# Sums of weight blocks made in DRAM scratch by accumulating transfers ahead of their stages, and nine more two by two steps, in a one-core transformer layer

## The chip, the cores and the metric

The kernel runs on one core of a Trainium2 chip. The time is the device time of one execution in microseconds (us). The kernel before took 716.37 us, the median of three runs (715.84 to 717.23).

Engines are named as the profile names them: PE multiplies matrices, DVE, ACT and POOL work on vectors, SP only issues transfers. Each engine runs its own instructions in a fixed order; an instruction that waits holds up all that stand behind it on its engine.

## The reference

One layer on 512 positions of width 1024, in float32:

```python
h = rms_norm(x, norm_mix_g[l])
proj = h @ w_in[l]                       # conv B, C, in | q, k, v | forget logits | gates
u = causal_dwconv(cc * cin, conv_mix_w[l])
y_conv = (cb * u) @ w_out_conv[l]
o = forgetting_attention(q, k, v, log_f) # 8 heads of 64
y_attn = o @ w_out_attn[l]
gates = jax.nn.sigmoid(g_logit + b_gate[l])
x = x + (g_conv * y_conv + g_attn * y_attn) @ w_o[l]
h = rms_norm(x, norm_ffn_g[l])
up = causal_dwconv(h @ w_up[l], conv_ffn_w[l])
a, b = jnp.split(up, 2, axis=-1)
x = x + (jax.nn.silu(a) * b) @ w_down[l]
return rms_norm(x, norm_f_g)
```

The hidden width is 2816, so that w_down is 22 by 8 blocks of 128 by 128.

## The kernel before, in words

**Products in three passes.** Everything lies with features on the partitions. A float32 product is made of three matmuls in a rounded format: each operand is split into hi (rounded) and lo (the rest), and hi·hi, lo·hi and hi·lo are summed in PSUM. One matmul takes a weight block of 128x128 and 256 positions. A plain product of four weight blocks (2 output by 2 input blocks) with both halves of the positions takes 8 such triples, 24 matmuls.

**Steps.** A *step* replaces these 8 products by 7 (21 matmuls): it multiplies sums and differences of the four weight blocks by sums and differences of the four input pieces, and adds results in the outputs. Seven weight forms are needed: three are plain blocks (the P chunk), four are sums (the F chunk). Two steps make a *double*. `seven` (L729) runs a list of doubles: chunk P is 18 matmuls (12 with the hi weights, then 6 with the lo weights), chunk F is 24 (16, then 8). Steps are used for the branch gates of output blocks j = 3 to 7 (`GATES`, two doubles each), and in the down projection. That runs in two phases, each behind its part of the up projection: hidden blocks 0 to 11 (phase 0, input pairs q = 0 to 5, 12 doubles) and 12 to 21 (phase 1, q = 6 to 10, 5 doubles), `STEPS`. In the lists (i, q) is output pair i with input pair q. What steps leave out in phase 1 is done in plain matmuls (`PLAIN`): outputs 2, 3, 6 and 7, in chunks dp0 to dp5.

**The weight stream.** All weights come through one list of chunks, `stream`. For each chunk SP loads `raw_*` (512 KB for 1024 columns), ACT makes the hi half `wh_*` (L237), DVE the lo half `wl_*` = raw - wh (L241). `wh` and `wl` have two buffers each, so a half of the next but one chunk waits until PE has read the one that lies there. `split` (L217) makes one chunk's halves while PE works on the chunk ahead of it.

**The sums.** For an F chunk SP loads half of the pieces to `raw_F` (256 KB), POOL adds the other half by an accumulating transfer (L187), and two POOL additions (L179, L180) make the last four of its eight columns of blocks, from `raw_F` itself and from `raw_P`. `sums`, `adds` and `forms` place them. ACT's hi half of an F chunk so waits for POOL.

**Side work.** Combining a step's outputs (`gate_pair`, `combine`), making the sums of the inputs (`x_sums`, `x_split` for the gates; `t13`, `t24` and `hl` in `glu` for the down projection) and the squares of the last norm (`final_square`) are entered in a list `later`, with a chunk from which they may run and a cost. After each split `run_later` (L198) issues as much of it as a budget of microseconds allows, and `flush` issues what a following step needs. So the order on DVE and ACT is fixed in the program, by the splits and these budgets.

**Names.** `xt`, `xth`, `xtl` are the sums of the normed input for the gates, with hi and lo halves; `xgh`, `xgl` the plain ones. `p_ga`, `p_gb` are gates of plain matmuls, `yc`, `ya` the two branch projections of a block j (chunk mix j), `g*`, `mh`, `ml` the merged branches. `dn*` are the PSUM banks of steps, `go`, `ge`, `gh`, `gl` the hidden activations and their forms, `pd`, `pdA`, `pdB` plain outputs of the down projection, `x`, `cz`, `cu` what combining writes. q10 is the last input pair of phase 1: its activations are made last, just before the steps.

Of the kernel before, what the change touches and what calls it, by code (L numbers as in the profile page):

```python
# [8 lines left out]
F32 = mybir.dt.float32  # L9
# [4 lines left out]
P = 128  # L14
# [34 lines left out]
    (((2, 6), (2, 7)), ((2, 8), (2, 9)), ((0, 6), (0, 7)), ((0, 8), (2, 10)), ((0, 9), (0, 10))),  # L49
# [11 lines left out]
def block_kernel(ctx, tc, xT, vecs, wv, win, wmix, wo, wup, wst, wdp, outT):  # L61
# [56 lines left out]
    def step_chunks(n):  # L118
        return [(f"P{n}", wst[n, :, : 6 * P], 6 * P), (f"F{n}", wst[n, :, 6 * P :], D)]
# [17 lines left out]
    raws, parts, order = [], [], {}  # L137
    later = []
    held = dict.fromkeys(NRAW, 0)
    stage = {"add": 0, "sum": 0}  # L140
# [11 lines left out]
    def load(upto):  # L152
        for k in range(len(raws), min(upto, len(stream) - 1) + 1):
            nm, src, ncol = stream[k]
            tag = tag_of(k)
            if held[tag] == NRAW[tag]:
                return
            held[tag] += 1
            pool = wp if tag == "raw" else fp if tag == "rf" else mp
            raw = pool.tile([P, D], F32, tag=tag, name=f"raw_{nm}", bufs=NRAW[tag])  # L160
# [13 lines left out]
    def sums(k, n):  # L174
        while stage["sum"] <= min(k + n, stage["add"] - 1):
            a = stage["sum"]
            if tag_of(a) != "raw":
                f, p = (raws[x].rearrange("p (a b) -> p a b", b=P) for x in (a, a - 1))
                keep(nc.gpsimd.tensor_add(f[:, 4:6], f[:, 0:4:2], p[:, 1:6:3]))  # L179
                keep(nc.gpsimd.tensor_add(f[:, 6:8], f[:, 4:6], p[:, 2:6:3]))  # L180
            stage["sum"] += 1

    def adds():
        while stage["add"] < len(raws):
            a = stage["add"]
            if tag_of(a) != "raw":
                keep(nc.gpsimd.dma_start(raws[a][:, : 4 * P], stream[a][1][:, 4 * P :], accum_op=ALU.add))  # L187
            stage["add"] += 1

    def forms(k):  # L190
        if k >= ff0:
            sums(k, 3)
            adds()
        else:
            adds()
            sums(k, 2)
# [20 lines left out]
    def split(hl=None):  # L217

        k = len(parts)
        if k == len(stream):  # L220
            return
        nm, _, ncol = stream[k]
        load(k + (LOOK if len(raws) > KB else AHEAD))
        forms(k)
        if hl is None:
            hl = []
            for x in "hl":
                if k == 0:
                    wp.tile([P, PADW[x]], F32, tag=f"pad{x}", name=f"pad_{x}")
                hl.append(wp.tile([P, D], F32R, tag=f"w{x}", name=f"w{x}_{nm}", bufs=2)[:, :ncol])  # L230
        hi, lo = hl
        raw = raws[k]
        if k == 0:
            for cs in (slice(0, VW), slice(VW, S + H)):
                keep(nc.vector.tensor_copy(hi[:, cs], raw[:, cs]))
        else:
            ins = nc.scalar.activation(hi, raw, AF.Copy)  # L237
            order["hi"] = ins.ins
            if k < KB:
                keep(ins)  # L240
        ins = nc.vector.tensor_sub(lo, raw, hi.bitcast(F32))  # L241
        order["lo"] = ins.ins
        if k < KB:
            keep(ins)
        held[tag_of(k)] -= 1
        assert tag_of(k) == "raw" or stage["sum"] > k
        parts.append((hi, lo))
        run_later(k, {"u": 1.7, "P": 1.6, "F": 0.75, "i": 3.0, "m": 3.0}.get(nm[0], 3.5))
# [452 lines left out]
    n = len(units)  # L701
    for i in range(n + LA):
        if i < n:
            scores(*units[i])
        take = 1 if i < n + LA - 1 else len(fill)
        for _ in range(min(take, len(fill))):
            fill.pop(0)()
        if 0 <= i - LT < n:
            transp(*units[i - LT])
        if 0 <= i - LA < n:  # L710
            pr, e, qb = units[i - LA]
            if e == 1 and qb % 2 == 1:
                attend(pr, qb // 2)
    at.close()
# [14 lines left out]
    def seven(doubles, n0, sets, operand, goes_on=None, stays=None, done=None):  # L729
# [3 lines left out]
        for n, d in enumerate(doubles):  # L733
            for kind in "PF":
                prods = []
                for s_, (i, q) in enumerate(d):
                    for f, g, b, h in PROD:
                        if (f < 3) == (kind == "P"):
                            wants.setdefault(f"{kind}{n0 + n}", []).append(("q", q))
                            c = 3 * s_ + f if f < 3 else 2 * s_ + f - 3 if f < 5 else 4 + s_ + 2 * (f - 5)  # L740
                            prods.append((c, i, operand(q, g), b, h))
# [33 lines left out]
    mp = mg.enter_context(tc.tile_pool(name="mp", bufs=1))  # L775
    mh = mp.tile([P, KB, S], F32R, tag="mh", name="mh")
# [43 lines left out]
    k = [c[0] for c in stream].index("mix1")  # L820
# [153 lines left out]
    fp = ctx.enter_context(tc.tile_pool(name="fp", bufs=1))  # L974
    fp.tile([P, PADL], F32, tag="pad", name="pad_f")
# [118 lines left out]
    for ph, (j0, j1) in enumerate(PHASES):  # L1094
        if ph:
            flush()
            acc = ring(*X)
        for j in range(j0, j1):
# [32 lines left out]
    def plain(m, t, ks, p, opens, closes):  # L1131
        for k in ks:
            while (m, k) not in where:
                fetch(plain.c)
                plain.c += 1
# [4 lines left out]
    plain.c = 0  # L1140
    for m, b in ((2, 4), (3, 2)):
        flush((b,))
        p = bank(b, f"pd{m}")
        for k in kall:
            for t in range(2):
# [10 lines left out]
    pdA, pdB6, pdB7 = bank(3, "pdA"), bank(5, "pdB6"), bank(0, "pdB7")  # L1156
# [56 lines left out]
def _layout(i):  # L1213
# [45 lines left out]
    for w4, d in [(wga, d) for d in GATES] + [(wdn, d) for d in STEPS[0] + STEPS[1]]:  # L1259
# [3 lines left out]
        w = pick((1, 1), (0, 0), (0, 1)) + pick((1, 0), (1, 0)) + pick((1, 1), (0, 0))  # L1263
        wst.append(np.concatenate(w, axis=1))
# [37 lines left out]
```

## Time and profile before

| | before |
|---|---|
| median of three runs | 716.37 us |
| the profiled execution | 716.79 us |
| its span in the trace | 715.0 us |
| PE, instructions | 6069 |
| DVE busy | 511.3 us |
| ACT busy | 334.0 us |
| POOL busy | 203.2 us |
| moved by DMA | 84.11 MB |

The span reaches from the first to the last instruction of the trace; the profiled execution is 1.8 us longer, start and end around it. A row of the timeline has start, length, engine, source line, operation, output and inputs; a bracket at its end says how long the engine was idle before and what it waited for. Matmuls overlap: their lengths are longer than the distance from one to the next, which is what counts.

### The profile page before, as it was taken

How to read it: one execution, taken by the hardware profiler on the slowest of the kernel's cores; microseconds unless marked ns; L12 is line 12 of the kernel's file. 1: busy time of each engine (PE TensorE's matmuls, PEld its weight loads, DVE VectorE, ACT ScalarE, POOL GpSimd, SP SyncE). 2: the span in 40 equal slices, each digit the busy share in tenths (PEclk: the TensorE clock that was granted, in tenths of full speed). 3: DMA queues.
4: the chain of work that ended last, by engine and by line, in shares of the span. 5: the costliest groups of instructions: out<-in, count | busy, mean ns of one | idle time of the engine just before them, and what ended most of it. 6: DMA issues, size and time to landing. Idle time of an engine off the chain costs nothing. (4 is left out here: it accounts for less than half of the span.)

```text
span 715.0 us, 14660 instructions
## 1 busy us (share of the span) xinstructions
PE 702.8 (98%) x6069; PEld 697.8 (98%) x6069; DVE 511.3 (72%) x758; ACT 334.0 (47%) x521; POOL 203.2 (28%) x222
## 2 busy tenths in 40 slices
PE   9999999999999999999999999999999999999996
PEld 9999999999999999999999999999999999999995
DVE  6677667675478888864468777779794677878963
ACT  5665545544464444343344444445433344444542
POOL 5124424222113444433301011045640111116202
PEclk9999999999999999999999999999999999999998
DMA  7423213122452656653313333357863233246313
GB/s 246 160 76 105 75 61 89 60 61 88 137 159 67 169 136 148 200 172 122 96 60 119 94 103 101 96 131 173 203 165 118 89 100 108 89 128 147 103 31 118
DMA packets 31571, 84.11 MB, mean 118 GB/s; under 512 B 3824, under 2 KB 6512, under 8 KB 31504
## 3 DMA queue, kind: packets, MB, share of 16 engines
q1 hardware_dynamic: 24736, 70.63, 31.1%
q0 software_dynamic: 5360, 11.31, 8.2%
q10 hardware_dynamic: 1408, 1.24, 0.5%
q8 instruction: 47, 0.77, 0.4%
q14 instruction: 20, 0.16, 0.1%
HBM read 81.00 MB, written 2.10 MB: 116 GB/s over the span
## 5 line engine op out<-in xcount | busy, mean ns | idle before, releaser
L269 PE MATMUL p_up<-x1h,wh_up 128*128 128x256 f32 x536 | 104.5, 276 | 0.0
L269 PE MATMUL p_up<-x1l,wh_up 128*128 128x256 f32 x536 | 104.4, 276 | 0.0
L269 PE MATMUL p_up<-x1h,wl_up 128*128 128x256 f32 x536 | 104.3, 276 | 0.0
L237 ACT ACTIVATE wh_up<-raw_up 128x1024 fp32r<-128x1024 f32 x44 | 46.7, 1060 | 89.1 <-PE p_up L269 68.8
L269 PEld LDWEIGHTS p_up<-x1h,wh_up 128*128 128x128 f32 x536 | 80.8, 188 | 0.0
L269 PEld LDWEIGHTS p_up<-x1l,wh_up 128*128 128x128 f32 x536 | 80.7, 188 | 0.0
L269 PEld LDWEIGHTS p_up<-x1h,wl_up 128*128 128x128 f32 x536 | 80.6, 188 | 0.0
L241 DVE TENSOR_TENSOR wl_up<-raw_up,wh_up 128x1024 fp32r<-128x1024 f32 x44 | 53.8, 1223 | 20.6 <-ACT wh_up L237 20.6
L269 PE MATMUL p_in<-xgh,wh_in 128*128 128x256 f32 x288 | 56.9, 279 | 1.0 <-ACT wh_in L237 1.0
L269 PE MATMUL p_in<-xgl,wh_in 128*128 128x256 f32 x288 | 56.5, 277 | 0.0
L269 PE MATMUL p_in<-xgh,wl_in 128*128 128x256 f32 x288 | 56.4, 277 | 0.0
L1008 POOL TENSOR_TENSOR ge<-fu,fu 128x512 f32<-128x512 f32 x11 | 17.1, 1551 | 124.2 <-DVE fu L519 111.3
L995 DVE TENSOR_TENSOR fz<-p_up,rb_n 128x512 f32<-128x512 f32 x44 | 30.3, 690 | 30.1 <-PE p_up L269 30.0
L269 PEld LDWEIGHTS p_in<-xgh,wh_in 128*128 128x128 f32 x288 | 44.7, 188 | 1.9 <-ACT wh_in L237 1.2
L241 DVE TENSOR_TENSOR wl_F<-raw_F,wh_F 128x1024 fp32r<-128x1024 f32 x27 | 39.6, 1468 | 8.7 <-ACT wh_F L237 8.1
L237 ACT ACTIVATE wh_F<-raw_F 128x1024 fp32r<-128x1024 f32 x27 | 28.6, 1061 | 33.7 <-PE dn L287 14.3
L269 PEld LDWEIGHTS p_in<-xgl,wh_in 128*128 128x128 f32 x288 | 43.6, 188 | 0.0
L269 PEld LDWEIGHTS p_in<-xgh,wl_in 128*128 128x128 f32 x288 | 43.5, 188 | 0.0
L287 PE MATMUL p_up<-x1h,wh_up 128*128 128x256 f32 x168 | 40.3, 277 | 0.0
L287 PE MATMUL p_up<-x1l,wh_up 128*128 128x256 f32 x168 | 40.2, 276 | 0.0
L241 DVE TENSOR_TENSOR wl_in<-raw_in,wh_in 128x1024 fp32r<-128x1024 f32 x26 | 33.2, 1276 | 9.6 <-ACT wh_in L237 9.1
L241 DVE TENSOR_TENSOR wl_P<-raw_P,wh_P 128x768 fp32r<-128x768 f32 x27 | 31.7, 1174 | 7.7 <-ACT wh_P L237 7.6
(315 smaller groups left out, 2127.2 us busy)
## 6 DMA issues: line engine op xcount, KB each, us to landing
raw_up<-in_wup_dram SPq DMA_DIRECT2D x44, 512.0 KB, 3.6
raw_in<-in_win_dram SPq DMA_DIRECT2D x26, 512.0 KB, 3.5
raw_P<-in_wst_dram SPq DMA_DIRECT2D x27, 384.0 KB, 3.2
raw_F<-in_wst_dram SPq DMA_DIRECT2D x27, 256.0 KB, 3.1
raw_F<-in_wst_dram POOLq DMA_DIRECT2D x27, 256.0 KB, 4.8
raw_mix<-in_wmix_dram SPq DMA_DIRECT2D x8, 512.0 KB, 4.8
raw_wo<-in_wo_dram SPq DMA_DIRECT2D x8, 512.0 KB, 6.7
xt<-in_xT_dram POOLq DMA_DIRECT2D x4, 512.0 KB, 6.4
```

The costliest lines, as they stand in the source:

```text
L237: ins = nc.scalar.activation(hi, raw, AF.Copy)
L241: ins = nc.vector.tensor_sub(lo, raw, hi.bitcast(F32))
L269: keep(nc.tensor.matmul(out[:, cs], w, x[:, cs], start=start and i == 0 and c == 0, stop=stop and i == 2 and c == len(cut) - 1,))
L287: keep(nc.tensor.matmul(out, wl if x == 1 else wh, xl if x == 2 else xh, start=opens and bk not in seen, stop=closes and bk not in left,))
L995: nc.vector.tensor_mul(z, p, rb2)
L1008: keep(nc.gpsimd.tensor_mul(ge, a.rearrange(halves_of, h=2), b.rearrange(halves_of, h=2)))
```

## The change

1. **The sums move into DRAM.** `make_forms` groups doubles and gives each group six transfers in DRAM scratch: SP copies pieces from `wst` there, POOL adds others by accumulating transfers (three copies, three additions, each waiting for the one ahead). `slot`, called once in each of the 37 turns of the attention loop and once for each up-projection block, issues what is due: the sums of the gates' 12 doubles during the attention (6 groups of 2, four slots from one transfer of a group to the next), those of phase 0 and phase 1 during the up projection ahead of them (groups of 4, two slots apart). SP then loads an F chunk like any other, 512 KB. `sums`, `adds` and `forms` go: 27 accumulating transfers and 54 additions of POOL. 36 accumulating transfers of POOL take their place (18 in the attention, 9 in each up projection), on 256 or 512 rows each instead of 128.
2. **Gates in steps from block 2** (`GJ`): two more doubles instead of plain matmuls. Their `xt` sums start a chunk earlier (`mix0` for `mix1`).
3. **Output pair 1 of phase 1 in steps**: two more doubles and one single step, (1, 10), at the end; `PLAIN` keeps outputs 6 and 7 (chunks dp0 to dp2). The order of the doubles changes: (2, 10) stands in the third instead of the fourth.
4. Banks of the last part are renumbered, and `wst` is padded to one width.

```diff
@@ tables @@
-    (((2, 6), (2, 7)), ((2, 8), (2, 9)), ((0, 6), (0, 7)), ((0, 8), (2, 10)), ((0, 9), (0, 10))),
+    (((2, 6), (2, 7)), ((2, 8), (2, 9)), ((2, 10), (0, 6)), ((0, 7), (0, 8)), ((0, 9), (0, 10)))
+    + (((1, 6), (1, 7)), ((1, 8), (1, 9)), ((1, 10),)),
-GJ = 3
+GJ = 2
-PLAIN = [(m, k) for m in (2, 3, 6, 7) for k in range(*PHASES[1])]
-PCUTS = (0, 8, 16, 20, 28, 32, 40)
+PLAIN = [(m, k) for m in (6, 7) for k in range(*PHASES[1])]
+PCUTS = (0, 8, 12, 20)
+DOUBLES = GATES + STEPS[0] + STEPS[1]
+GROUPS = {"gate": (2, 4, 1), 0: (4, 2, 4), 1: (4, 2, 3)}
@@ load @@
-            elif tag != "raw":
-                keep(nc.sync.dma_start(raw[:, : 4 * P], src[:, : 4 * P]))
             else:
-                keep(nc.sync.dma_start(raw[:, :ncol], src))
+                keep(nc.sync.dma_start(raw[:, :ncol], src if tag == "raw" else made[src]))
...
-                keep(nc.gpsimd.tensor_add(f[:, 4:6], f[:, 0:4:2], p[:, 1:6:3]))
-                keep(nc.gpsimd.tensor_add(f[:, 6:8], f[:, 4:6], p[:, 2:6:3]))
...
-                keep(nc.gpsimd.dma_start(raws[a][:, : 4 * P], stream[a][1][:, 4 * P :], accum_op=ALU.add))
...
+    def make_forms(n0, n1, key):
+        size, step, shift = GROUPS[key]
...
+            m = len(DOUBLES[a]) * P
+            f = dr.tile([P, b - a, 4 * m], F32, tag=f"f{a}", name=f"f{a}")
+            w = wst[a:b].rearrange("n p c -> p n c")
+            x0, x1, x2 = w[:, :, 3 * m : 5 * m], w[:, :, 5 * m : 7 * m], w[:, :, 7 * m : 8 * m]
...
+            def put(dst, src):
+                return lambda: keep(nc.sync.dma_start(dst, src))
+            def add(dst, src):
+                return lambda: keep(nc.gpsimd.dma_start(dst, src, accum_op=ALU.add))
+            f0, f1, f2 = f[:, :, : 2 * m], f[:, :, 2 * m : 3 * m], f[:, :, 3 * m :]
+            ops = (put(f0, x0), add(f0, x1), put(f1, f[:, :, :m]), add(f1, x1[:, :, m:]), put(f2, f1), add(f2, x2))
+            todo_bg.extend((make_forms.slot + step * k + shift * g, op) for k, op in enumerate(ops))
...
+    def slot():
+        while todo_bg and todo_bg[0][0] <= make_forms.slot:
+            todo_bg.pop(0)[1]()
+        make_forms.slot += 1
@@ attention loop, up @@
+    make_forms(0, len(GATES), "gate")
     for i in range(n + LA):
+        slot()
...
         for s_ in range(2):
+            slot()
@@ gates @@
-    k = [c[0] for c in stream].index("mix1")
+    k = [c[0] for c in stream].index("mix0")
@@ the last part @@
-    for m, b in ((2, 4), (3, 2)):
...
-                plain(m, t, (k,), p[:, th[t]], t == 0, t == 1)
-        nc.vector.tensor_add(x1[:, m, :], p, x1[:, m, :])
-        later.append((0, 0.8, (), lambda m=m: final_square(m)))
...
-    fetch(3)
+    fetch(0)
-    fetch(4, [wx[:, a : a + 4 * P] for a in (80, 752)])
-    fetch(5)
+    fetch(1, [wx[:, a : a + 4 * P] for a in (80, 752)])
+    fetch(2)
```

**What moves on the engines.** Below, a row has the source line (in the kernel after, most lines stand 13 to 18 further down), the operation, output and inputs with their numbers, and the shape. P0, F0, P1, F1 are the four chunks of block j = 2 after the change (of j = 3 before it).

ACT after, from the split of chunk F0 of block 2 on:

```order
L250 ACTIVATE wh_F0_2883<-raw_F0_2719 128x1024
L918 ACTIVATE mh_2595<-g1_2743 128x512
L250 ACTIVATE wh_P1_2915<-raw_P1_2721 128x768
L250 ACTIVATE wh_F1_2943<-raw_F1_2723 128x1024
L831 ACTIVATE xth_2590<-xt_2589 128x1024 x2
L250 ACTIVATE wh_mix2_2975<-raw_mix2_2733 128x1024
```

DVE after, at the same place:

```order
L919 TENSOR_TENSOR ml_2596<-g1_2743,mh_2595 128x512
L254 TENSOR_TENSOR wl_P1_2916<-raw_P1_2721,wh_P1_2915 128x768
L824 SCALAR_TENSOR_TENSOR xt_2589<-xt_2589 128x2x256
L825 SCALAR_TENSOR_TENSOR xt_2589<-xt_2589 128x2x256
L254 TENSOR_TENSOR wl_F1_2944<-raw_F1_2723,wh_F1_2943 128x1024
L832 TENSOR_TENSOR xtl_2591<-xt_2589,xth_2590 128x1024 x2
L254 TENSOR_TENSOR wl_mix2_2976<-raw_mix2_2733,wh_mix2_2975 128x1024
```

DVE before, where the same sums of inputs q = 2 and 3 were made, ahead of block 3's first chunk:

```order
L903 TENSOR_TENSOR ml_2552<-g1_2691,mh_2551 128x512
L804 TENSOR_TENSOR xt_2545<-xt_2545 128x2x256
L805 TENSOR_TENSOR xt_2545<-xt_2545 128x2x256
L808 SCALAR_TENSOR_TENSOR xt_2545<-xt_2545 128x2x256
L809 SCALAR_TENSOR_TENSOR xt_2545<-xt_2545 128x2x256
L241 TENSOR_TENSOR wl_mix2_2881<-raw_mix2_2681,wh_mix2_2880 128x1024
L816 TENSOR_TENSOR xtl_2547<-xt_2545,xth_2546 128x1024 x2
L241 TENSOR_TENSOR wl_P0_2943<-raw_P0_2743,wh_P0_2942 128x768
```

Before, the last sums and both halves of inputs 2 and 3 stood ahead of the first step chunk. Now they stand behind the splits of P1 and F1, the chunks that read them.

DVE before, at the steps of phase 1, where the forms of q10 (`go10`, `gl`) are made; P25 is the chunk that reads them first:

```order
L241 TENSOR_TENSOR wl_F23_8186<-raw_F23_7958,wh_F23_8185 128x1024
L1025 TENSOR_TENSOR go10_8095<-ge10_7954 128x256
L1026 TENSOR_TENSOR go10_8095<-go10_8095,ge10_7954 128x256
L241 TENSOR_TENSOR wl_P24_8218<-raw_P24_8026,wh_P24_8217 128x768
L1029 SCALAR_TENSOR_TENSOR go10_8095<-go10_8095 128x256
L1035 TENSOR_TENSOR gl_4468<-ge10_7954,gh_4467 128x2x256
L1030 SCALAR_TENSOR_TENSOR go10_8095<-go10_8095 128x256
L241 TENSOR_TENSOR wl_F24_8250<-raw_F24_8028,wh_F24_8249 128x1024
L1035 TENSOR_TENSOR gl_4468<-go10_8095,gh_4467 128x512
L241 TENSOR_TENSOR wl_P25_8282<-raw_P25_8096,wh_P25_8281 128x768
L1035 TENSOR_TENSOR gl_4468<-go10_8095,gh_4467 128x512 x2
```

DVE after, at the same place (two doubles more stand ahead of it in the count, so that 25 and 26 are the second and the third double of the phase); P26 reads them first:

```order
L254 TENSOR_TENSOR wl_F25_8205<-raw_F25_7987,wh_F25_8204 128x1024
L1043 TENSOR_TENSOR go10_8120<-ge10_7983 128x256
L1044 TENSOR_TENSOR go10_8120<-go10_8120,ge10_7983 128x256
L254 TENSOR_TENSOR wl_P26_8237<-raw_P26_8052,wh_P26_8236 128x768
L1047 SCALAR_TENSOR_TENSOR go10_8120<-go10_8120 128x256
L1053 TENSOR_TENSOR gl_4492<-ge10_7983,gh_4491 128x2x256
L1048 SCALAR_TENSOR_TENSOR go10_8120<-go10_8120 128x256
L1053 TENSOR_TENSOR gl_4492<-go10_8120,gh_4491 128x512 x2
L254 TENSOR_TENSOR wl_F26_8275<-raw_F26_8054,wh_F26_8274 128x1024
L1053 TENSOR_TENSOR gl_4492<-go10_8120,gh_4491 128x512
```

The forms themselves keep their place on DVE; the chunk that reads them has come a double closer to the front.

DVE before, at the end of the steps, where the plain chunks begin (pair 1 is not in steps there):

```order
L241 TENSOR_TENSOR wl_F26_8366<-raw_F26_8155,wh_F26_8365 128x1024
L1055 TENSOR_TENSOR cz12_8341<-dn1024_6628,cz12_8341 128x256
L1063 TENSOR_TENSOR x1_3961<-dn1023_6627,x1_3961 128x256
L1062 TENSOR_TENSOR cu12_8369<-dn1025_6629,cz12_8341 128x256
L241 TENSOR_TENSOR wl_dp0_8398<-raw_dp0_8183,wh_dp0_8397 128x1024
```

DVE after, there: F31 is the single step (1, 10), `cz11`, `cu11` and the rows between them combine pair 1.

```order
L254 TENSOR_TENSOR wl_F31_8558<-raw_F31_8363,wh_F31_8557 128x512
L1107 TENSOR_TENSOR ssq3_4493<-ssq3_4493,sq3_0_8561 128x512
L254 TENSOR_TENSOR wl_dp0_8578<-raw_dp0_8389,wh_dp0_8577 128x1024
L1107 TENSOR_TENSOR ssq3_4493<-ssq3_4493,sq3_1_8581 128x512
L1076 TENSOR_TENSOR x1_3985<-dn2412_8430,x1_3985 128x512
L1073 TENSOR_TENSOR cz11_8585<-dn2414_8432,cz11_8585 128x256
L1081 TENSOR_TENSOR x1_3985<-dn2413_8431,x1_3985 128x256
L1080 TENSOR_TENSOR cu11_8589<-dn2415_8433,cz11_8585 128x256
L1084 TENSOR_TENSOR x1_3985<-x1_3985,dn2413_8431 128x512
L1087 TENSOR_TENSOR x1_3985<-x1_3985,cz11_8585 128x512
L1091 TENSOR_TENSOR x1_3985<-x1_3985,cu11_8589 128x512
L254 TENSOR_TENSOR wl_dp2_8607<-raw_dp2_8511,wh_dp2_8606 128x1024
```

Before, plain chunks of 8 to 16 matmul triples followed the last combination; now the seven rows of pair 1's combination stand between the splits of dp0 and dp2.

More of the change, by code (lines that the diff above doesn't have):

```diff
@@ L137, in block_kernel @@
     raws, parts, order = [], [], {}
+    pools = {"raw": wp}
     later = []
     held = dict.fromkeys(NRAW, 0)
-    stage = {"add": 0, "sum": 0}
     def after_split():
@@ L155, in load @@
             tag = tag_of(k)
[L156 removed]
+            if held[tag] == NRAW[tag] or tag not in pools:
                 return
             held[tag] += 1
[L159 to L160 removed]
+            raw = pools[tag].tile([P, D], F32, tag=tag, name=f"raw_{nm}", bufs=NRAW[tag])
             if k == 0:
@@ L183, in adds @@
[L183 to L196, printed above, removed]
+    dr = ctx.enter_context(tc.tile_pool(name="dr", bufs=1, space=bass.MemoryType.DRAM))
+    made, todo_bg = {}, []
@@ L713, in block_kernel @@
                 attend(pr, qb // 2)
+    assert not todo_bg
     at.close()
```

50 lines of the change are left out of this document (26 added, 24 removed).

## The prediction

> **What bounds the kernel now.** First the page's table of engines, then the chain that ended last.
>
> ```profile
> PE 702.8 (98%) x6069; PEld 697.8 (98%) x6069; DVE 511.3 (72%) x758; ACT 334.0 (47%) x521; POOL 203.2 (28%) x222
> 676.46 13.60 PE pd L269 x120
> 690.06 6.80 PE pdA L269 x60
> ```
>
> PE is busy 98% of the span. In the chain, stretches without a wait give the price of a matmul: 13.60/120 = 6.80/60 = 0.1133 us. (The 0.28 us that a row shows is a pipelined length.) So time goes with the number of matmuls, plus the stalls that are hidden in the 98%. The windows of the stages with steps show those, set against their matmul counts (start, length, then busy times):
>
> ```profile
> 227.51:307.19 79.68, 78.41 (x663) 76.07 (x661) 69.45 (x76) 34.89 (x46) 36.76 (x35) 1.00 0.56 155
> 650.53:676.30 25.77, 24.74 (x213) 24.15 (x211) 23.53 (x28) 13.33 (x17) 10.34 (x10) 1.00 0.55 129
> ```
>
> Gates j = 3 to 7 are 5 blocks of 132 matmuls: 660 x 0.1133 = 74.78 us, and took 79.68: **4.90 us of stalls**. Phase 1's steps are 210 x 0.1133 = 23.79 us and took 25.77: **1.98 us**. In phase 0's steps there are two stalls:
>
> ```profile
> 491.71 0.28 PE L287 MATMUL dn<-gl,wh_F 128*128 128x256 f32 x1
> 492.33 0.50 PE L287 MATMUL dn<-gh,wl_F 128*128 128x256 f32 x2 [0.35 <-DVE wl_F L241]
> 499.39 0.28 PE L287 MATMUL dn<-gl,wh_P 128*128 128x256 f32 x1
> 500.12 0.50 PE L287 MATMUL dn<-gh,wl_P 128*128 128x256 f32 x2 [0.45 <-DVE wl_P L241]
> ```
>
> Of the distance of 0.62, one 0.11 is no stall, but the matmul behind it came 0.11 late again, so 0.62 is lost; likewise 0.73: **1.35 us**. All together 8.2 us. Who causes them:
>
> ```profile
> L237 ACT ACTIVATE wh_F<-raw_F 128x1024 fp32r<-128x1024 f32 x27 | 28.6, 1061 | 33.7 <-PE dn L287 14.3 <-POOL raw_F L180 14.1 <-DVE wl_F L241 2.4
> L241 DVE TENSOR_TENSOR wl_F<-raw_F,wh_F 128x1024 fp32r<-128x1024 f32 x27 | 39.6, 1468 | 8.7 <-ACT wh_F L237 8.1 <-PE dn L287 0.6
> L241 DVE TENSOR_TENSOR wl_up<-raw_up,wh_up 128x1024 fp32r<-128x1024 f32 x44 | 53.8, 1223 | 20.6 <-ACT wh_up L237 20.6
> 293.24 1.28 POOL L901 TENSOR_TENSOR ga<-ga,gb 128x512 f32<-128x512 f32 x1 [2.11 <-DVE gb L900]
> 293.42 2.19 DVE L241 TENSOR_TENSOR wl_F<-raw_F,wh_F 128x1024 fp32r<-128x1024 f32 x1 [0.26 <-ACT wh_F L237]
> 293.44 0.39 PE L287 MATMUL dn<-xgh,wh_F 128*128 128x256 f32 x1 [0.63 <-ACT wh_F L237]
> ```
>
> ACT waited 14.1 us for POOL's sums, and PE then for ACT (293.44). And the lo half of an F chunk takes 1.468 us on average against 1.223 for the same shape in the up projection: where POOL works beside it, it takes up to 2.19. At 293.42 it ends 1.09 us after POOL's addition (293.24 + 1.28 = 294.52), about its undisturbed length.
>
> The Trainium skill, "SBUF — State Buffer", section "Who interferes with whom", says that a DVE instruction with two SBUF inputs contends with a GpSimd instruction that reads SBUF, and that the order of issue decides who blocks. The rows above agree: POOL came first, DVE waited it out. By that rule the sum below is 714.4 where POOL issues first in block 2, and 715.4 where DVE does.
>
> **The change part by part**, against the profiled execution, 716.79 us (0.42 above the median of 716.37).
>
> *Matmuls.* Four gate steps and five pair-1 steps save 3 matmuls each: 9 x 3 x 0.1133 = **-3.06 us**.
>
> *Old stalls.* 54 POOL additions and their waits go, ACT's hi halves wait for a load alone. For a gate block I follow the order of DVE and ACT undisturbed: F0's lo half, beside the merge's POOL addition, is there 3.2 us after the block starts and wanted after 34 matmuls, 3.85; P1's 5.0 against 6.1; F1's 7.3 against 8.6. Every chunk has over 0.6 us to spare. In phases 0 and 1 the shorter lo halves do it. **-4.90, -1.35, -1.98 us**; that they stay is a rival below.
>
> *Block j = 2.* The new order puts the last `xt` sums behind P1's lo half and the `xtl` behind F1's, though P1 reads them. Rows for the walk, on before's clock:
>
> ```profile
> 199.14 1.23 DVE L241 TENSOR_TENSOR wl_in<-raw_in,wh_in 128x1024 fp32r<-128x1024 f32 x1 [3.31 <-ACT wh_in L237]
> 206.86 0.69 DVE L809 SCALAR_TENSOR_TENSOR xt<-xt 128x512 f32<-128x512 f32 x1
> 207.58 2.01 ACT L815 ACTIVATE xth<-xt 128x1024 fp32r<-128x1024 f32 x2 [0.38 <-DVE xt L809]
> 208.68 2.36 DVE L816 TENSOR_TENSOR xtl<-xt,xth 128x1024 fp32r<-128x1024 f32 x2
> 211.19 0.39 PE L269 MATMUL p_ga<-xgh,wh_in 128*128 128x256 f32 x2
> 211.68 0.72 ACT L786 ACTIVATE g<-g,vec 128x512 f32<-128x512 f32 x1 [2.08 <-DVE g L785]
> 225.71 0.96 DVE L241 TENSOR_TENSOR wl_P<-raw_P,wh_P 128x768 fp32r<-128x768 f32 x1 [1.52 <-ACT wh_P L237]
> 230.15 0.64 ACT L902 ACTIVATE mh<-g 128x512 fp32r<-128x512 f32 x1 [1.17 <-POOL g L901]
> ```
>
> P0 takes p_ga's place at 211.19. Without a stall P1 would end 84 - 24 = 60 matmuls later, at 217.99. DVE, from wl_in at 199.14 on: four sums, ml and the mix lo half to 205.1, two xtl to 207.5, then between the sigmoids P0's lo half (210.7), two sums and the two merge products to 213.9. POOL's merge addition then runs to 215.2 and F0's lo half beside it to 216.1; ml to 216.8, P1's lo half to 217.8, the two sums to 219.2, F1's lo half to 220.4, xtl to 221.6 and 222.8. PE ends F0 at 216.1 + 8 x 0.1133 = 217.0 (1.0 late), does P1's hi passes up to the twelfth, which needs the second xtl, and six lo passes: 223.6. Stall **+5.6 us**. If DVE's lo half issues ahead of POOL's addition, mh comes 1.1 later and all behind it: +6.6. If F0 isn't held up at all, P1 still waits for the same rows: +4.6. I take 5.6.
>
> *q10 in the third double.* P26 starts 84 matmuls into the steps, 650.53 + 9.52 = 660.05, and wants its sixth operand, the last piece of `gl`, at 660.62.
>
> ```profile
> 655.80 1.11 DVE L1015 TENSOR_TENSOR go<-fu,fu 128x512 f32<-128x512 f32 x1
> 660.18 0.95 DVE L241 TENSOR_TENSOR wl_P<-raw_P,wh_P 128x768 fp32r<-128x768 f32 x1
> 661.05 0.41 DVE L1029 SCALAR_TENSOR_TENSOR go<-go 128x256 f32<-128x256 f32 x1
> 661.38 0.68 DVE L1035 TENSOR_TENSOR gl<-ge,gh 128x512 fp32r<-128x512 f32 x1
> 667.88 0.38 PE L287 MATMUL dn<-gl,wh_P 128*128 128x256 f32 x1 [0.66 <-DVE gl L1035]
> ```
>
> From 655.80 DVE has, by the distances of undisturbed rows, the product 0.6, F25's lo half 1.15, two sums 0.65, P26's lo half 0.9, a sum 0.35, gl 0.6, a sum 0.35, two gl 1.3: 661.7. That is 1.1 late; F26 adds about 0.1. **+1.2 us**. The row at 667.88 shows the same wait in the fourth double already, 0.8 with the contention of then; so 0.4 to 1.6.
>
> *The end.* Pair 1's single step covers less (F31: 12 matmuls, 1.36 us).
>
> ```profile
> 675.59 1.06 ACT L237 ACTIVATE wh_dp<-raw_dp 128x1024 fp32r<-128x1024 f32 x1 [1.43 <-PE dn L287]
> 677.14 1.22 DVE L241 TENSOR_TENSOR wl_dp<-raw_dp,wh_dp 128x1024 fp32r<-128x1024 f32 x1
> 677.45 0.72 ACT L1090 ACTIVATE x<-x,vec 128x512 f32<-128x512 f32 x1
> 678.07 0.62 ACT L1088 ACTIVATE sq<-x 128x512 f32<-128x512 f32 x1
> 678.61 0.68 DVE L1058 TENSOR_TENSOR x<-dn,x 128x512 f32<-128x512 f32 x1
> ```
>
> With T the end of F30: ACT makes F31's hi half to T-0.25, a square and a copy to T+1.0, dp0's hi half to 2.1; its lo half on DVE ends at 3.3. The plain chunk's second matmul wants it at T + 1.02 + 1.36 + 0.11 = 2.5: 0.9 late with the restart. dp2's lo half then stands behind a square's sum and the seven rows of pair 1's combination (0.6 for one of 512, 0.33 for one of 256), 7.6 to 8.85; wanted 36 matmuls after dp0's, at 7.5. **+2.3 us** in all; 1 if only the first wait shows, 3 if the banks are read late too.
>
> *At nothing.* 18 accumulating transfers of POOL in the attention and 18 in the up projections, with as many copies on SP.
>
> ```profile
> DMA  7423213122452656653313333357863233246313
> L187 POOL DMA_DIRECT2D raw_F<-in_wst_dram x27 | 23.8, 904 | 43.1 <-DMA raw_F<-in_wst_dram 17.0 <-DVE ga L850 9.1 <-DVE ga L855 5.2
> raw_F<-in_wst_dram SPq DMA_DIRECT2D x27, 256.0 KB, 3.1
> raw_F<-in_wst_dram POOLq DMA_DIRECT2D x27, 256.0 KB, 4.8
> L1008 POOL TENSOR_TENSOR ge<-fu,fu 128x512 f32<-128x512 f32 x11 | 17.1, 1551 | 124.2 <-DVE fu L519 111.3
> POOL pp L574 <- DVE m L573: 41.4, 18, 4.2
> ACT ych L547 <- POOL y L546: 10.0, 4, 2.9
> ```
>
> Before 18 of the 32 pp instructions of the attention POOL stood idle, 41.4 us in all. An issue took 0.904 us for 128 rows; for 256 rows I estimate twice that, 1.8 us (bounds 0.9, as for 128, and 3.6), 18 x 1.8 = 33 us, which lie in those 41.4. In the up projections POOL was idle 124.2 us before 11 products alone. A copy and an addition of 256 KB landed in 3.1 and 4.8 us; in DRAM neither was seen. Between one transfer of a group and the next lie two up blocks of 48 matmuls, 10.9 us, or four attention turns, which is more than twice the slower of the two. About 1 MB more per double moves while the row of DMA shares stands mostly at 1 to 6 tenths. If this cover is gone, SP's next raw load or POOL's next pp is late: the second rival prices it.
>
> Sum: 716.79 - 3.06 - 4.90 - 1.35 - 1.98 + 5.6 + 1.2 + 2.3 = 714.6, on the median's basis 0.42 less, 714.2. One more small restart at each of the three new waits is possible; I say **714.4 us**.
>
> **The rivals.** *The new waits are small.* The scheduler's order is fixed, but my walk is late by construction where an engine is ahead of before's clock: DVE had 3.31 us idle before 199.14, and 27 x 0.245 = 6.6 us of contention on wl_F go. With block 2's wait at 2, q10 at 0.4 and the end at 1, the time is 716.37 - 11.29 + 3.4 = 708.5. Against it: P1's wait hangs on the row order, not on when DVE got there.
>
> *POOL's issues delay the attention* (slower). POOL's y gates ACT's ych (10.0 us waited in four times), and pp gates the transposes. If an issue of 1.8 us stands ahead of y four times, and ACT's lateness goes through to PE, that is +7.2: 714.4 + 7.2 = 721.6; with 3.6 us an issue, 728.8. It decides from the point where the issue outlasts what ACT and PE have in hand. For it: ACT waits there already. The Trainium skill, in the section named above, also says that POOL's making of descriptors can be starved by DVE; the 904 ns of L187, beside a DVE busy 72%, show none of it, and by that rule the time would lie nearer 728.8. Against it: PE shows no wait for pth or ych in the attention now.
>
> *The old stalls stay* (the change doesn't do what it says): if ACT's and DVE's own order, and not POOL, held PE, the 8.2 us return: 714.4 + 8.2 = 722.6. For it: at 667.88 PE waited for gl, no weight at all, and 14.3 us of ACT's idle time before wh_F came from PE itself. Against it: 293.44.
>
> **How the numbers follow.** The forecast has 0.62: the bounds of its terms (4.6 to 6.6, 0.4 to 1.6, 1 to 3) give 711.3 to 716.5, and a part of the old stalls that stays gives up to 718. A measurement tells some 0.2% from no change, 714.9 to 717.8. Of the forecast I put 0.38 below, 0.23 within, 0.01 above. Small new waits 0.14, all faster. The attention 0.14 and the old stalls 0.10; most of both lies above 717.8, 0.02 within. So faster 0.52, same 0.25, slower 0.23. For 8 in 10 the range reaches a good way to the rivals on both sides: 709.5 to 719.5; the forecast's own is 711.3 to 718.
>
> **What would show it.** In the profile after: 27 PE instructions fewer than before, but for missing records; no POOL additions on raw_F, wh_F waiting for PE or a load; wl_F at about 1.23 us; gate blocks from 3 on at 14.96 us each. In block 2 two waits of PE, on wl_F0 (about 1 us) and on xtl (about 4.6), P1 ending some 12.4 us after P0 starts; in phase 1 a wait on gl in the third double; at the end waits on wl_dp twice. Wrong would be: PE waiting on tp, pth or ych in the attention (second rival), raw_F loads held by SP behind a copy that waits, or gate blocks still over 15.5 us (third).

## The result, and the profile after

| | before | after |
|---|---|---|
| median of 4 runs | 716.41 us | 735.78 us |
| ratio to before | | 1.0261, 95% interval 1.0236 to 1.0287 |
| the profiled execution, its span | 716.79, 715.0 us | 735.92, 734.1 us |
| DMA moved | 84.11 MB | 118.91 MB |

The change makes the kernel 2.6% slower, above the range of 709.5 to 719.5 us. One execution of a later kernel (the sums alone), 1005 us at a granted clock of 0.65 from end to end, is left out below. The page of the changed kernel starts so:

```profile
PE 705.7 (96%) x6042; PEld 700.8 (95%) x6042; DVE 498.0 (68%) x773; ACT 338.5 (46%) x528; POOL 163.9 (22%) x177
```

PE has 27 instructions fewer, as expected, and is busy 3 us longer in a span 19 us longer. The next view, windows over the stages (start:end, length, busy times, granted PE clock, DMA share, GB/s), shows where. First the kernel before: gates, first up projection, steps of phase 0.

```profile
189.36:307.19 117.83, 116.56 (x999) 114.22 (x998) 96.64 (x107) 56.07 (x73) 45.21 (x45) 1.00 0.55 155
350.71:483.21 132.50, 132.50 (x1171) 132.50 (x1169) 96.13 (x136) 59.79 (x83) 23.26 (x18) 1.00 0.33 100
483.21:541.73 58.52, 57.72 (x507) 57.32 (x506) 48.99 (x57) 27.14 (x33) 29.40 (x31) 1.00 0.69 173
```

The same stages after, and the steps of phase 1:

```profile
188.37:308.62 120.25, 114.72 (x987) 113.56 (x986) 88.97 (x114) 58.91 (x76) 13.50 (x15) 0.99 0.49 160
352.14:500.70 148.56, 138.25 (x1170) 137.26 (x1169) 96.34 (x136) 59.66 (x83) 29.00 (x22) 0.97 0.68 181
500.70:557.82 57.12, 57.12 (x506) 57.12 (x505) 42.44 (x57) 27.07 (x33) 0.00 (x0) 1.00 0.58 178
666.62:706.52 39.90, 38.27 (x317) 37.67 (x316) 30.47 (x45) 21.90 (x31) 0.00 (x0) 0.96 0.34 105
```

**The first up projection took 16.1 us more** (148.56 against 132.50), a stage in which the change computes nothing else. The gates took 2.4 more, though they have 12 matmuls fewer. Phase 0's steps fell to 57.12 us, 504 matmuls without a stall. Phase 1's steps took 39.90 for 315 matmuls (35.70 without a stall). In the attention and the second up projection nothing changed (136.0 and 108.8 us in both). The time is 21.4 us above the forecast of 714.4. By stages, each against what was forecast for it, that is 16.1 us in the first up projection, 3.1 in the gates and 3.2 from the steps of phase 1 to the end; the part ahead of the gates was 1.0 shorter.

What PE and SP waited for after (engine, line, releaser: us in all, times, longest), and the row of ACT's hi halves:

```profile
PE p_up L299 <- ACT wh_up L250: 10.2, 3, 5.5
PE p_gb L281 <- ACT wh_in L250: 2.1, 1, 2.1
PE pdA L281 <- DVE wl_dp L254: 1.6, 2, 0.8
PE dn L299 <- DVE gl L1053: 1.4, 1, 1.4
PE dn L299 <- ACT xth L831: 1.2, 1, 1.2
ACT wh_up L250 <- DMA raw_up<-in_wup_dram: 22.3, 4, 8.0
SPq L194 <- DMA f<-in_wst_dram: 162.1, 21, 20.9
L250 ACT ACTIVATE wh_F<-raw_F 128x1024 fp32r<-128x1024 f32 (+1 forms) x32 | 33.7, 1052 | 32.9 <-PE dn L299 26.6
```

The last row shows that the wait for POOL's sums is gone. The two above it show what came in its place: SP stood 162 us at copies in scratch (L194), waiting for POOL's accumulating transfers, and ACT waited 22 us for raw_up. The timeline of the longest of the three stalls, from POOL to PE:

```profile
397.31 1.61 POOL L1026 TENSOR_TENSOR ge<-fu,fu 128x512 f32<-128x512 f32 x1 [15.86 <-DVE fu L531]
398.86 2.37 POOL L197 DMA_DIRECT2D f<-in_wst_dram  x2
405.24 6.73 SPq L194 DMA_DIRECT2D f<-f  x2
412.01 0.63 SPq L194 DMA_DIRECT2D f<-in_wst_dram  x1
412.75 2.54 SPq L170 DMA_DIRECT2D raw_up<-in_wup_dram  x4
420.89 1.06 ACT L250 ACTIVATE wh_up<-raw_up 128x1024 fp32r<-128x1024 f32 x1 [8.04 <-DMA raw_up<-in_wup_dram]
422.00 0.58 PE L299 MATMUL p_up<-x1h,wh_up 128*128 128x256 f32 x1 [5.49 <-ACT wh_up L250]
```

POOL sat idle 15.86 us at the product ge, which needs the last DVE result of its block. Its two additions stand behind that product, so they went out at 398.86. SP's copies wait for them: the first could go at 405.24, the second at 411.49. Behind the copies on SP stand four loads of raw_up, which left together from 412.75 on; the first was of use at 420.89, and PE stood still for 5.5 us.

### The profile page after: what moved, and what is told of

The parts are those of the page before. It is cut to its first block, busy times and chain, and to the rows that moved or that the text cites. A ratio compares the mean times of both kernels' runs of the same rounds, so it can differ in the third digit from the quotient of the medians.

```text
span 734.1 us, 14600 instructions
## 1 busy us (share of the span) xinstructions
PE 705.7 (96%) x6042; PEld 700.8 (95%) x6042; DVE 498.0 (68%) x773; ACT 338.5 (46%) x528; POOL 163.9 (22%) x177
## 2 busy tenths in 40 slices
DMA packets 54130, 118.91 MB, mean 162 GB/s; under 512 B 4624, under 2 KB 24080, under 8 KB 54064
## 5 line engine op out<-in xcount | busy, mean ns | idle before, releaser
L281 PE MATMUL p_up<-x1h,wh_up 128*128 128x256 f32 x536 | 105.8, 279 | 0.0
L281 PE MATMUL p_up<-x1l,wh_up 128*128 128x256 f32 x536 | 105.3, 278 | 0.0
L254 DVE TENSOR_TENSOR wl_up<-raw_up,wh_up 128x1024 fp32r<-128x1024 f32 x44 | 55.6, 1264 | 42.6 <-ACT wh_up L250 42.6
L281 PEld LDWEIGHTS p_up<-x1h,wh_up 128*128 128x128 f32 x536 | 82.1, 191 | 0.0
L281 PEld LDWEIGHTS p_up<-x1h,wl_up 128*128 128x128 f32 x536 | 82.1, 190 | 0.0
L254 DVE TENSOR_TENSOR wl_F<-raw_F,wh_F 128x1024 fp32r<-128x1024 f32 (+1 forms) x32 | 43.7, 1365 | 14.8 <-ACT wh_F L250 14.8
L299 PE MATMUL p_up<-x1h,wh_up 128*128 128x256 f32 x168 | 41.4, 282 | 10.2 <-ACT wh_up L250 10.2
L250 ACT ACTIVATE wh_F<-raw_F 128x1024 fp32r<-128x1024 f32 (+1 forms) x32 | 33.7, 1052 | 32.9 <-PE dn L299 26.6
L197 POOL DMA_DIRECT2D f<-in_wst_dram x36 | 47.3, 1436 | 0.1
L299 PEld LDWEIGHTS p_up<-x1h,wh_up 128*128 128x128 f32 x168 | 32.1, 191 | 10.8 <-ACT wh_up L250 10.8
L250 ACT ACTIVATE wh_P<-raw_P 128x768 fp32r<-128x768 f32 (+1 forms) x32 | 26.6, 832 | 31.1 <-PE dn L299 22.7
```

The source lines that it names most:

```text
L197: return lambda: keep(nc.gpsimd.dma_start(dst, src, accum_op=ALU.add))
L281: keep(nc.tensor.matmul(out[:, cs], w, x[:, cs], start=start and i == 0 and c == 0, stop=stop and i == 2 and c == len(cut) - 1,))
L299: keep(nc.tensor.matmul(out, wl if x == 1 else wh, xl if x == 2 else xh, start=opens and bk not in seen, stop=closes and bk not in left,))
```

## The experiments

**Is it SP's queue, or the traffic?** Theory A: the raw loads wait behind the copies. Theory B: 35 MB more in the same memory slow them. Three kernels tell these apart. The first two change only the distance of the transfers in phase 0:

```diff
-GROUPS = {"gate": (2, 4, 1), 0: (4, 2, 4), 1: (4, 2, 3)}
+GROUPS = {"gate": (2, 4, 1), 0: (4, 4, 1), 1: (4, 2, 3)}     # four slots
+GROUPS = {"gate": (2, 4, 1), 0: (4, 3, 4), 1: (4, 2, 3)}     # three slots
```

> Edit: in phase 0 the six transfers of a group stand four slots apart instead of two (all three groups together), the bytes are the same. Theory A (queue order): SP's copy from scratch to scratch waits for POOL's addition, which stands behind a product on POOL, and the raw loads of the up projection wait behind the copy on SP. Then two more blocks (10.9 us) of distance take most of the wait away: the first up projection falls from 148.6 us to 132.5 to 135, the time from 735.8 to 720 to 723. Theory B (traffic): the loads are late because of the 32 MB more that move; then the stage stays at 146 to 150 and the time at 733 to 737.

> Edit: the changed kernel with phase 0's transfers three slots apart instead of two, the groups where they were. A size between the two tried. If SP's wait for POOL is what delays the loads, each of the three stalls (2.0, 5.5 and 3 us) is shortened by up to one block of 5.4: stage 132.5 to 134 us, time 720 to 722. If only the grouping of the four-slot run helped (all copies early), it stays above 140.

Measured: 721.36 us with four slots (ratio to before 1.0072, 95% interval 1.0050 to 1.0095), 719.92 with three (1.0052, 1.0033 to 1.0072). The stage with four slots, and SP's wait; then the stage with three:

```profile
353.97:486.47 132.50, 132.50 (x1171) 132.50 (x1170) 95.39 (x136) 59.78 (x83) 28.92 (x22) 1.00 0.71 190
SPq L194 <- DMA f<-in_wst_dram: 109.8, 22, 17.1
```

```profile
354.14:486.64 132.50, 132.50 (x1171) 132.50 (x1170) 95.39 (x136) 59.79 (x83) 28.69 (x22) 1.00 0.75 199
```

The stage is back at 132.50 us with more traffic per microsecond than before (190 GB/s against 181). SP still waits 110 us for POOL, but now no raw load that PE needs stands behind it for too long. With three slots the stage took 132.50 us too, at 199 GB/s. A holds; B doesn't.

The third takes the copies out: SP copies only first terms from the weights, POOL adds every other one.

```diff
-ops = (put(f0, x0), add(f0, x1), put(f1, f[:, :, :m]), add(f1, x1[:, :, m:]), put(f2, f1), add(f2, x2))
+ops = ((0, put(f0, x0)), (0, put(f1, xa)), (0, put(f2, xa)), (1, add(f0, x1)), (1, add(f1, ya)), (1, add(f2, ya)))
+ops += ((3, add(f1, yb)), (3, add(f2, yb)), (5, add(f2, x2)))
```

> Edit: no copy from scratch to scratch. SP copies all first terms from the weights at once, waiting for nothing, and POOL adds the others, one by one, with 27 percent more bytes and 72 accumulating transfers instead of 36. Theory A (SP's copies wait for POOL): first up projection 132.5 to 134 us, time 719 to 722, and no wait of SP for an addition ahead of a raw load of an up block. Theory B (traffic): no better than 148 us in that stage, time 735 or above.

Measured: 743.07 us (1.0374, 1.0344 to 1.0404), so the forecast of the time failed, but that of the stage held: the first up projection took 132.5 us, at 238 GB/s and a DMA share of 0.96, which speaks against B once more. The loss had moved to the attention, 156.3 us against 136.0. This kernel's waits show where:

```profile
PE tp L604 <- POOL pp L588: 15.2, 2, 10.6
```

In the attention POOL had 36 additions instead of 18. Many wait for an addition ahead of them (14.3 us in 11 waits over the whole kernel) and hold up pp, which the transposes need. Other waits of POOL beside the longest stall are put down to a weight load, so how much is due to the additions' waits for one another, and how much to issuing them, is not shown. The engine and the place are those of the prediction's second rival, at double the load; in the changed kernel PE waits for no pp.

**Block 2's gates.** Steps from block 3 again:

```diff
-GJ = 2
+GJ = 3
-    k = [c[0] for c in stream].index("mix0")
+    k = [c[0] for c in stream].index("mix1")
```

> Edit: gates in steps from block 3 again, with the sums of the inputs where they stood before. Theory C: block 2 in steps costs 4.5 us in block 1 (the loads of raw_F, sent as soon as the attention's memory is free, share the DMA engines with xt, and ACT waits for xt ahead of p_gb's weights) and 4.1 us in chunk P0 and P1, and saves 1.4; so the gate stage falls from 120.3 to 113 us and the time from 735.8 to 728 to 729. Rival D: block 1's wait is a backlog of SP from the attention's copies; then only P0's and P1's part goes, gate stage 117.5, time 732 to 733.

Measured: 729.99 us (1.0191, 1.0162 to 1.0221); gate stage 113.94 us instead of 120.25. So block 2 in steps costs 6.3 us here, its saved 1.4 us counted in. That is near C's figure; the wait for wh_in ahead of p_gb went with it. To see whether xt comes late because of the loads beside it, a hold on SP's raw_F loads was tried first; then the two loads were put on POOL's queue behind xt.

```diff
-            if held[tag] == NRAW[tag] or tag not in pools:
+            if held[tag] == NRAW[tag] or tag not in pools or (tag == "rg" and k > len(parts) + 2):
...
+                eng = nc.gpsimd if tag == "rg" and src < 2 else nc.sync     # only in the second
```

> Edit: the run with four slots (721.4), and in the gates the loads of raw_F, and what stands behind them, are sent only two chunks ahead, so that they no longer go out beside the loads of xt. If block 1's wait (p_gb, 3.2 us and PE at half speed behind it) comes from xt landing late beside raw_F: xt lands in 6 to 7.5 us as before, the wait goes, gate stage from 121.9 to 117 to 118, time 717. If ACT or SP is late there for another reason: stage 121 to 122, time 721.

> Edit: the run with four slots (721.4), with block 2's two loads of raw_F issued from POOL's queue behind xt (holding them on SP's queue moved nothing: they went out at the same time). If xt is late because 1.4 MB of other loads share the DMA engines with its 2 MB (at 362 GB/s in the window of 194 to 198 us), 1 MB less beside it brings it 2 to 2.7 us earlier: xt lands in 6 to 8.3 us, PE's wait for wh_in ahead of p_gb goes from 2.3 to under 0.5, gate stage from 121.9 to 117 to 119, time 717 to 719. If the lateness isn't the traffic's: 121 to 122, time 721.

The hold moved nothing in time (SP sent raw_F at 189.3 us, at once when the attention's memory was free): 721.0 us, xt still 10.0 us to landing. It tells nothing of the cause. On POOL's queue the loads did move. The landing of xt (page of DMA issues), after and in this run, and this run's waits of PE:

```profile
xt<-in_xT_dram POOLq DMA_DIRECT2D x4, 512.0 KB, 9.8
```

```profile
xt<-in_xT_dram POOLq DMA_DIRECT2D x4, 512.0 KB, 6.5
212.56 0.38 PE L300 MATMUL dn<-xgh,wh_P 128*128 128x256 f32 x1 [1.14 <-DVE g L916]
222.82 0.58 PE L300 MATMUL dn<-xth,wh_P 128*128 128x256 f32 x1 [4.56 <-ACT xth L832]
224.26 0.58 PE L300 MATMUL dn<-xtl,wh_P 128*128 128x256 f32 x1 [0.87 <-DVE xtl L833]
```

xt landed in 6.5 us as before, and the wait ahead of p_gb is gone: the loads beside it were its cause. But the gate stage took 121.8 us, no less (721.8 us in all): PE now waits 6.6 us in block 2 itself. Part of that is the edit's own. POOL sends the load of raw_F for F1 only behind its addition in the merge, and on ACT xth stands behind the hi half that waits for this load:

```profile
215.37 0.57 POOL L171 DMA_DIRECT2D raw_F<-f  x1
218.44 0.69 DVE L826 SCALAR_TENSOR_TENSOR xt<-xt 128x512 f32<-128x512 f32 x1
220.76 1.06 ACT L251 ACTIVATE wh_F<-raw_F 128x1024 fp32r<-128x1024 f32 x1 [3.94 <-DMA raw_F<-f]
221.72 1.99 ACT L832 ACTIVATE xth<-xt 128x1024 fp32r<-128x1024 f32 x2
```

The last sum that xth reads was there at 219.13, and xth began at 221.72. By an estimate from these rows some 2.6 of the 6.6 us come from the moved load. What block 2 costs with xt and raw_F both on time, no run shows. Another order of the same rows:

```diff
-run_later(k, {"u": 1.7, "P": 1.6, "F": 0.75, "i": 3.0, "m": 3.0}.get(nm[0], 3.5))
+run_later(k, {"u": 1.7, "P": 1.6, "F": 0.75, "i": 3.0, "m": 3.0}.get(nm[0], 3.5) if nm != "P0" else 6.0)
```

> Edit: the run with four slots, with the whole of the sums and halves of inputs 2 and 3 behind the split of P0 (a budget of 6 us there), so that they stand ahead of F0's, P1's and F1's splits on DVE. If P1's 4.1 us in block 2 are due to the order of these rows, P1 no longer waits for xth or xtl; DVE has the same work to do, so F0's lo half comes some 3 us later, and PE waits there instead: gate stage 120 to 121.5 (121.9), time 719.5 to 721. If DVE's load doesn't bound the block, the whole wait goes: 118, time 717.

Measured: 720.01 us (1.0062, 1.0042 to 1.0082), gate stage 120.4 (121.9). P1 no longer waits, P0 and F0 do. The three longest distances between matmuls in block 2 were 0.72, 1.54 and 1.26 us and are now 1.51, 1.36 and 0.52: 3.2 and 3.1 us above a matmul's 0.1133. So the waits hardly became shorter. Most of the 1.5 us won is another thing: with four slots PE ran at half clock behind these waits (granted clock 0.50 from 224.4 to 227.7 us), here at full clock. The order of the rows sets where the wait shows, and not how long it is; what sets its length, no run separates.

**Phase 1 and the end.** Pair 1 plain again, with the list of steps, `PLAIN`, `PCUTS` and the last part of before:

```diff
-    (((2, 6), (2, 7)), ((2, 8), (2, 9)), ((2, 10), (0, 6)), ((0, 7), (0, 8)), ((0, 9), (0, 10)))
-    + (((1, 6), (1, 7)), ((1, 8), (1, 9)), ((1, 10),)),
+    (((2, 6), (2, 7)), ((2, 8), (2, 9)), ((0, 6), (0, 7)), ((0, 8), (2, 10)), ((0, 9), (0, 10))),
-PLAIN = [(m, k) for m in (6, 7) for k in range(*PHASES[1])]
+PLAIN = [(m, k) for m in (2, 3, 6, 7) for k in range(*PHASES[1])]
```

> Edit: output pair 1 of phase 1 in plain matmuls again, the doubles of phase 1 in the order of before, (2, 10) in the fourth. Theory E: the waits of phase 1 (q10 2.3 us and 1.8 us of PE at half speed behind it, the end 2.1 us) come from the order of the steps; the part from the first step of phase 1 on falls from 67.5 to 62.5 to 63.5 us, the time from 735.8 to 731 to 732. Rival F: they come from phase 1's sums in scratch (late loads of raw_F); then that part is no shorter than before's 64.5 and the time 733 or above.

Measured: 731.82 us (1.0217, 1.0187 to 1.0247). From the first step of phase 1 on 62.6 us instead of 67.5, E's figure. So pair 1 in steps, in the changed order of doubles, saves 15 matmuls, 1.7 us, and costs 4.8 net of that.

Two kernels tried to keep the steps and lose the waits, with gates from block 3, four slots and (2, 10) in the fourth double. The first puts all side work behind dp2's split; the second moves the single step ahead of pair 1's other doubles.

```diff
+        last = nm[0] == "d" or nm == f"F{len(DOUBLES) - 1}"
+        run_later(k, 0.0 if last else {"u": 1.7, "P": 1.6, ...}.get(nm[0], 3.5))
```

```diff
-    + (((1, 6), (1, 7)), ((1, 8), (1, 9)), ((1, 10),)),
+    + (((1, 10),), ((1, 6), (1, 7)), ((1, 8), (1, 9))),
...
+   "d": 0.0                                       # in the budgets
```

> Edit: as the run with the sums alone, but pair 1 of phase 1 in steps, (2, 10) back in the fourth double, and the side work of the last step and of the plain chunks put behind dp2's split. If q10's place and the rows ahead of dp0's and dp2's splits cause all that is lost in phase 1 and at the end: steps of phase 1 35.7 to 36.3 us (39.7 in the changed kernel), the part behind them 25.2 to 26.2 (27.6), the time 707.5 to 709. If either has another cause, its stage stays at 39.7 or 27.6 and the time at 710 to 713.

> Edit: sums in scratch with four slots, gates from block 3, (2, 10) in the fourth double, the single step (1, 10) moved ahead of the other two doubles of pair 1, so that a whole double (F: 24 matmuls, 2.7 us) covers the first plain chunk, and no side work ahead of dp2's split. If the short cover and the rows ahead of dp2 caused the end's two waits: no wait on wl_dp, the part behind the steps 25.2 to 26.5 us (27.6 in the changed kernel, 29.7 with the side work only put off), steps of phase 1 35.7, time 707 to 709. If the single step leaves a wait wherever it stands: steps of phase 1 above 36.5.

Measured: 711.18 us (six runs from 709.67 to 713.68; 0.9934, 0.9911 to 0.9958) and 711.58 (0.9941, 0.9926 to 0.9956), both slower than expected. In the first the steps of phase 1 took 35.70 us, not a stall: q10's place was the whole of that loss. The part behind them took 29.7 us. Its waits, then those of the second:

```profile
PE pc_n L315 <- DVE ssq L1182: 1.8, 1, 1.8
PE pdA L282 <- DVE wl_dp L254: 0.6, 1, 0.6
```

```profile
PE pc_n L314 <- DVE ssq L1181: 1.6, 1, 1.6
PE dn L299 <- ACT wh_F L250: 0.9, 1, 0.9
```

The side work that was put off is late for the last norm instead (pc_n reads ssq), and the single step leaves a wait wherever it stands, at dp0 or at the next F chunk. In the second the steps took 37.1 and the rest 28.5 us.

**The sums alone.** What is left when block 2, pair 1 and phase 0's two slots are undone:

> Edit: the sums in DRAM scratch alone, with phase 0's transfers four slots apart; gates in steps from block 3, pair 1 of phase 1 plain as before. If the losses found so far are all there is: gate stage 113.9 us (before 117.8), first up projection 132.5, steps of phase 0 57.1 (before 58.5), steps of phase 1 23.8 (before 25.8), everything else as before, so 716.4 - 3.9 - 1.4 - 2.0 = 709.1, faster than both kernels. If the traffic of the sums costs something by itself wherever it runs, 712 or above.

> The sums in scratch alone once more, for its profile at full clock: 708.5 us, gate stage 113.7 to 114, first up projection 132.5, steps of phase 0 57.1, steps of phase 1 23.8, the part behind them 38.8.

Measured: 708.41 us, the median of three (0.9896, 0.9875 to 0.9916) and, the same kernel again, 708.73 (0.9904, 0.9887 to 0.9920). This beats both kernels, by 1.0% before and 3.7% after. Its gates, first up projection, steps of phase 0 and of phase 1:

```profile
188.77:302.86 114.09, 113.33 (x998) 113.12 (x998) 85.14 (x107) 56.80 (x73) 13.50 (x15) 1.00 0.49 161
346.38:478.88 132.50, 132.50 (x1170) 132.50 (x1169) 95.39 (x136) 59.90 (x83) 28.93 (x22) 1.00 0.71 192
478.88:536.00 57.12, 57.12 (x507) 57.12 (x505) 42.43 (x57) 27.07 (x33) 0.00 (x0) 1.00 0.66 203
644.80:668.60 23.80, 23.80 (x213) 23.80 (x211) 19.86 (x28) 13.34 (x17) 0.00 (x0) 1.00 0.33 101
```

Every step stage runs at 0.1133 us a matmul but for 1.2 us in the gates.

## Why the prediction was wrong

**The step that failed is "at nothing".** The prediction gave the copies and additions in the up projection a cover of two blocks, 10.9 us, "more than twice the slower of the two". Slots are places in the program, and two engines run past them at different times. SP is ahead of PE by as many raw loads as it has buffers, four; POOL is behind, because ge, which stands ahead of its additions, waits for the end of a block on DVE. So the copy came to wait for an addition not yet sent, up to 20.9 us. The landing was longer than the row of before as well: 8.8 us for an addition of 512 KB in scratch, against 4.8 for one of 256 KB to raw_F. The prediction did say which load would be late if the cover were gone, but priced only POOL's side of it, in the attention. The runs with three and four slots show the price: 16.1 us, all of it gone with the distance.

Part of these 16.1 us is a second term that the sum lacked: after the longer stalls PE ran at half its clock. The windows around the stall at 422 us (the third number from the end is the granted clock):

```profile
416.00:422.00 6.00, 0.51 (x6) 0.32 (x4) 0.02 (x1) 1.11 (x2) 0.00 (x0) 0.90 1.02 381
422.00:427.60 5.60, 5.60 (x26) 5.60 (x27) 5.60 (x7) 3.27 (x5) 2.33 (x3) 0.50 0.27 108
427.60:433.00 5.40, 5.40 (x49) 5.40 (x49) 3.99 (x6) 2.31 (x3) 2.76 (x3) 1.00 0.88 121
```

26 matmuls in 5.60 us stand against 49 in 5.40. Over the stage such stretches cost 4.5 us (45 distances of 0.2 us or more below 0.3, each less 0.1133), the three stalls and their restarts 11.4.

Point by point:

- *Matmuls, -3.06 us:* 27 fewer, right by count.
- *Old stalls, -8.2 us:* right. Phase 0's steps have none left (-1.40), and those of phase 1 none where pair 1 is plain (-1.97). The gate stage of the kernel with the sums alone became 3.7 us shorter, out of 4.97 above its matmuls' time. The 1.2 us that it is still above lie in block 1, not in the steps, and are new: xt landed in 7.5 us instead of 6.4, and p_gb waits 0.8 us for wl_in. Why xt came later there no run shows. So the third rival falls.
- *Block 2, +5.6 us:* near in size, and in part by luck. Steps in block 2 cost 6.3 us net of the 1.4 us of matmuls that they save, so 7.7. But the first wait stands where the walk had none: 2.1 us ahead of p_gb, because xt lands late beside the loads of raw_F that block 2 sends out. The prediction didn't follow the moved loads there. The waits in block 2 itself come to 3.1 us by the distances, for xth and xtl, where the walk had 4.6 to 6.6, since PE came late already; the walk's wait on wl_F0 isn't there. Half clock made 1.4 us of the stage. With xt on time PE waited 6.6 us in block 2, the size for the prediction's other order of issue, but that run's own late load is in it.
- *q10, +1.2 us:* the wait is where it was put; its size was off. The rows, whose brackets hold 0.21 and 1.36 us:

```profile
677.30 0.38 PE L299 MATMUL dn<-gh,wh_P 128*128 128x256 f32 x1 [0.21 <-ACT gh L1052]
679.05 0.39 PE L299 MATMUL dn<-gl,wh_P 128*128 128x256 f32 x1 [1.36 <-DVE gl L1053]
```

  The waits and restarts come to 2.3 us, half clock behind them to 1.7; with some small delays that is 4.2 in the stage. The cause is a row that the walk misplaced. It let all of gl be made ahead of F26's lo half; but the last piece, for which P26 waited, stands behind that half on DVE, in the order shown ahead of the prediction already:

```profile
675.97 1.28 DVE L1053 TENSOR_TENSOR gl<-go,gh 128x512 fp32r<-128x512 f32 x2
677.18 1.22 DVE L254 TENSOR_TENSOR wl_F<-raw_F,wh_F 128x1024 fp32r<-128x1024 f32 x1
678.31 0.68 DVE L1053 TENSOR_TENSOR gl<-go,gh 128x512 fp32r<-128x512 f32 x1
```

- *The end, +2.3 us:* right, in place and size: two waits on wl_dp, the distances 1.09 and 1.03 us, each with a restart of 0.1.

The rival of POOL in the attention didn't come true in the changed kernel: the attention took 136.0 us as before, and PE waited for no pp. An issue of POOL took 1.18 us in the median of 36, less than the 1.8 that the prediction estimated. Only with twice the additions did PE wait there.

## What to carry to other kernels

Work that is "issued ahead" runs at the time of the queue it stands in. For every transfer between two queues, ask how far ahead of the bottleneck the waiting queue runs, how far behind the other one does, and what stands behind the wait: here three slots instead of two were worth 16 us with the same bytes. A saving of a few matmuls wasn't worth a shorter chunk where the chunk was what covered the next split, and moving side work that is needed soon only moved the wait.

## What was not expected of the hardware

- PE's clock fell to half after short stalls. Behind 1.89 and 2.05 us between two matmuls (the waits for ssq at the end in the two runs with pair 1 kept) there followed some 3 us at half clock; in the changed kernel behind the 2.38, 3.27 and 5.76 us between matmuls too, and behind q10's 0.59 and 1.75, but not behind the 1.99 us at 394 us. In the run with three slots q10's wait is as long as with four (1.74 and 1.75 us) and no half clock follows (granted clock of the stage 1.00 and 0.96): steps of phase 1 38.2 and 39.7 us. That is about the difference between their times, 719.9 and 721.4. So some 1.5 us between two runs can be half clock alone. The run with all side work behind dp2, around its last wait:

```profile
691.95:693.90 1.95, 1.95 (x16) 1.95 (x17) 0.16 (x1) 0.50 (x2) 0.65 (x1) 0.96 0.00 0
693.90:697.20 3.30, 3.30 (x18) 3.30 (x17) 0.68 (x2) 0.67 (x2) 0.27 (x2) 0.51 0.00 0
697.20:701.00 3.80, 3.77 (x34) 3.68 (x33) 2.45 (x6) 0.76 (x3) 1.09 (x1) 1.00 0.68 237
```

  The Trainium skill, "TensorE: Matmul & The Clock Gate", section "Part 1: The HAM clock gate (the "warmup" mystery)", says that an idle window of some 3.4 us brings the half rate. The half rate agrees (0.50 and 0.51); the length doesn't, as pauses of 1.9 to 2.1 us were enough here. What decides between the pauses that cost nothing and those of the same length that did was not tried.
- 35 MB more over the span cost PE nothing in the steps and up projections by itself: with the sums alone the steps of phase 0 ran at 203 GB/s and 0.1133 us a matmul, and without copies from scratch the first up projection took its 132.5 us at 238 GB/s.
